# An encoder kernel at 272 tokens: the layer norm between two layers done in place on fp32 sums, its evacuations given priority, weights split in pairs

## The chip, the core and the metric

One Trainium2 chip, one of its cores. TensorE (PE) multiplies, VectorE (DVE), ScalarE (ACT) and GpSimd (POOL) work on tiles of 128 partitions, and DMA queues bring the weights. The metric is the device time of one execution in microseconds (us).

## The reference

Four layers of a post-norm encoder, on 256 tokens and 16 meta tokens, width 2048. The mixers are neighbourhood attention (A), differential attention (B), sliding-window attention with grouped keys (C), and A again. Each takes its projections q, k, v, z from one matrix, gates its output by silu(z) and goes through an output matrix. Everything is fp32.

```python
for i in range(DEPTH):
    y = mixer_i(h, w_in)
    out = jnp.einsum('ble,ed->bld', y, w_out[i])
    h = _layer_norm(DEEPNORM_ALPHA * h + out, ln_g[i], ln_b[i])
```

## The kernel before

Everything is held transposed: features on partitions, 272 tokens along the row, 16 tiles of 128 features (k-tiles). A product of fp32 quality is three matmuls (`mm3`, L148 to L150) of values split into a high part (rounded to fp32r) and the rest: hi·hi, lo·hi, hi·lo. Activations are split where they are made. Weights are streamed from HBM and split on the way: `split_to` takes a granule (4 k-tiles by 128 columns), ACT writes wh (L156), DVE writes wl = raw − wh (L157), both 128x512. The splits run up to 8 granules ahead of PE. A granule is 12 matmuls, an output tile of 128 features 48.

An order of granules is written out by `granules`; `run` walks through it and emits the matmuls of one granule at each step, then one step of each side task (attention of a head, evacuations, residual, norm). From this program a scheduler that simulates the engines sets each engine's queue, so a queue's order isn't the order of the code. PSUM has three banks for accumulators (acc, taken in turn), two for scores and column sums (sc), two for transposes (tr), one for attention outputs (o).

At the end of a layer, `on_out` (L706) adds the residual to an output tile (`residual`: L693 on POOL adds the two halves of h, then ACT scales by alpha). `accum` takes a pivot off, splits d·g into uh and ul (with two more columns that hold the norm's gain and bias, from which the matmul makes two column sums of the weights), and keeps running sums of d and d² on POOL (L753, L754). After the last of the 16 tiles `norm_stats` makes the column sums on PE, then negmu (L776), variance, Ln and Exp on ACT, and one Newton step on DVE, whose last instruction is L784 (rstd).

So that PE needn't wait for that, the first seven input tiles of the next layer (DEFERRED) are multiplied with the un-normalised uh, ul. `rows` corrects them at their evacuation: a copy of the two extra columns (gb, two buffers, L308), an STT on DVE that reads the accumulator and adds negmu times the first (L310), and a multiplication by rstd on POOL (L314). ACT and DVE then write the two halves (for q and k: L322, L332), from which the scores are made. All other input tiles need the normalised h: `normalise` forms it for each k-tile by adding uh and ul on POOL (L797), an STT on DVE (L798), a multiplication by rstd on POOL (L799), and a split on ACT and DVE (L802, L803). `exact` is the mark that the first normalised granule has been reached. At the very end `norm_last` normalises the output with L820 and later lines and stores it.

(An STT is a scalar_tensor_tensor, one DVE instruction with two tensors and a scalar.)

## Time and profile before

| | us |
|---|---|
| median of 3 runs (lowest to highest) | 2007.85 (2006.71 to 2008.03) |
| the profiled execution | 2007.29 |
| its span | 2005.5 |
| PE busy | 1957.6 (98%) |
| DVE busy | 1456.4 (73%) |
| ACT busy | 1105.0 (55%) |
| POOL busy | 677.1 (34%) |

The chain of work that ended last is PE for 93% and DVE for 5%. The mean granted clock of PE is 0.991 of full. Busy times are of the profiled execution; what lies around its span is 1.8 us.

### The profile page before, as it was taken

The page shows a single profiled execution, that of the slowest core. Times are in us where ns is not written, and L with a number is a line of the kernel's source. Part 1 is how long each engine was busy: PE and PEld are TensorE (multiplying, and loading weights), DVE is VectorE, ACT ScalarE, POOL GpSimd, SP SyncE. Part 2 cuts the span into 40 slices and gives each one's busy share as a digit, 9 for nine tenths or more (in the row PEclk, how much of TensorE's full clock was granted, in tenths as well). Part 3 has the DMA queues.
Part 4 walks back from the last instruction along what each step waited for, and adds up shares of the span by engine and source line. Part 5 has one row for each costly group of instructions (what it writes and reads, how often), then busy time and mean ns, then how long its engine had stood idle before and what let it go on. Part 6 is the DMA issues. An engine that isn't in the chain of part 4 may idle for free.

```text
span 2005.5 us, 40741 instructions
## 1 busy us (share of the span) xinstructions
PE 1957.6 (98%) x15794; PEld 1948.7 (97%) x15794; DVE 1456.4 (73%) x2617; ACT 1105.0 (55%) x2396; POOL 677.1 (34%) x947
## 2 busy tenths in 40 slices
PE   9999999999989999999999899999998999999995
PEld 9999999999989999999999899999998999999995
DVE  7666666667998777777779977766898666666665
ACT  6555555555656555555555655655555555555553
POOL 2110011118683122212396832324965111111084
PEclk9999999999999999999999999999999999999998
DMA  8444454444534444444445344444444444445442
GB/s 277 172 155 176 155 176 155 173 148 160 199 121 154 149 167 148 167 155 160 154 151 188 109 163 150 148 151 172 149 172 155 171 167 170 171 176 175 159 165 78
DMA packets 52466, 324.00 MB, mean 162 GB/s; under 512 B 5904, under 2 KB 12064, under 8 KB 14768
## 3 DMA queue, kind: packets, MB, share of 16 engines
q1 hardware_dynamic: 51984, 320.76, 44.8%
q8 instruction: 124, 2.03, 0.4%
q14 instruction: 70, 0.57, 0.1%
q0 software_dynamic: 288, 0.63, 0.1%
HBM read 319.27 MB, written 2.10 MB: 160 GB/s over the span
## 4 chain that ended last, share of the span: by engine, by line
PE 93%; DVE 5%; issue 1%; POOL 1%; DMA 0%; ACT 0%; SPq 0%; DVEq 0%; POOLq 0%
PE acc L148 28%; PE acc L150 28%; PE acc L149 28%; DVE wl L157 1%; PE sc L150 1%; PE sc L148 1%; PE sc L149 1%; PE o L150 1%; PE o L149 1%; DVE ht L798 1%; PE o L148 1%; PE tr L464 1%; PE tr L472 1%; DVE yl L803 0%; DVE yl L822 0%
## 5 line engine op out<-in xcount | busy, mean ns | idle before, releaser
L157 DVE TENSOR_TENSOR wl<-raw,wh 128x512 fp32r<-128x512 f32 x1184 | 904.2, 770 | 435.8 <-ACT wh L156 424.0
L156 ACT CAST wh<-raw 128x512 fp32r<-128x512 f32 x1184 | 721.8, 618 | 609.8 <-PE acc L149 584.6
L148 PE MATMUL acc<-yh,wh 128*128 128x272 f32 (+2 forms) x2448 | 702.1, 287 | 0.0
L149 PE MATMUL acc<-yl,wh 128*128 128x272 f32 (+2 forms) x2448 | 701.8, 287 | 0.0
L150 PE MATMUL acc<-yh,wl 128*128 128x272 f32 (+2 forms) x2448 | 700.7, 286 | 0.0
L148 PE MATMUL acc<-hh,wh 128*128 128x272 f32 (+3 forms) x2288 | 664.8, 291 | 5.4 <-ACT wh L156 5.3
L150 PE MATMUL acc<-hh,wl 128*128 128x272 f32 (+3 forms) x2288 | 663.7, 290 | 0.2 <-DVE wl L157 0.2
L149 PE MATMUL acc<-hl,wh 128*128 128x272 f32 (+3 forms) x2288 | 662.5, 290 | 1.0 <-DVE hl L157 1.0
L148 PEld LDWEIGHTS acc<-yh,wh 128*128 128x128 f32 x2448 | 461.0, 188 | 0.3
L149 PEld LDWEIGHTS acc<-yl,wh 128*128 128x128 f32 x2448 | 460.9, 188 | 0.1
L150 PEld LDWEIGHTS acc<-yh,wl 128*128 128x128 f32 x2448 | 460.7, 188 | 0.0
L148 PEld LDWEIGHTS acc<-hh,wh 128*128 128x128 f32 x2288 | 434.7, 190 | 6.1 <-ACT wh L156 5.8
L149 PEld LDWEIGHTS acc<-hl,wh 128*128 128x128 f32 x2288 | 433.8, 190 | 1.3 <-DVE hl L157 1.3
L150 PEld LDWEIGHTS acc<-hh,wl 128*128 128x128 f32 x2288 | 434.1, 190 | 0.5 <-DVE wl L157 0.4
L346 DVE RECIPROCAL ez<-ez 128x272 f32<-128x272 f32 (+1 forms) x64 | 116.7, 1824 | 24.4 <-POOL ez L344 24.4
L347 POOL TENSOR_TENSOR gate<-gate,ez 128x272 f32<-128x272 f32 (+1 forms) x64 | 66.0, 1031 | 109.8 <-DVE ez L346 107.8
L407 POOL MEMSET vs<- 128x16 f32 x32 | 3.6, 113 | 236.5 <-PE tr L472 215.1
L344 POOL TENSOR_SCALAR ez<-ez 128x272 f32<-128x272 f32 (+1 forms) x64 | 27.3, 427 | 162.0 <-ACT ez L343 161.8
L419 POOL MEMSET s<- 128x16 f32 x32 | 3.6, 114 | 191.8 <-PE tr L469 163.2
L754 POOL TENSOR_TENSOR os<-os,sq 128x272 f32<-128x272 f32 (+1 forms) x59 | 62.9, 1066 | 0.0
L799 POOL TENSOR_TENSOR ht<-ht,rstd 128x272 f32<-128x272 f32 x48 | 50.9, 1073 | 26.2 <-DVE rstd L784 15.6
L753 POOL TENSOR_TENSOR os<-os,r 128x272 f32<-128x272 f32 x45 | 47.7, 1060 | 20.0 <-DVE r L706 20.0
(278 smaller groups left out, 2095.8 us busy)
## 6 DMA issues: line engine op xcount, KB each, us to landing
raw<-in_wts SPq DMA_DIRECT2D x293, 1024.0 KB, 4.8
bias<-in_bias_a SPq DMA_DIRECT2D x32, 184.0 KB, 2.3
raw<-in_wts SPq DMA_DIRECT2D x12, 256.0 KB, 5.4
yh<-in_xT SPq DMA_DIRECT2D x16, 136.0 KB, 4.9
out_h<-raw SPq DMA_DIRECT2D x8, 256.0 KB, 2.1
dist<-in_dist_b POOLq DMA_DIRECT2D x1, 272.0 KB, 6.9
dist<-in_dist_c POOLq DMA_DIRECT2D x1, 272.0 KB, 4.8
lnp<-in_lnp POOLq DMA_DIRECT2D x1, 64.0 KB, 4.2
```

The source lines that it names most:

```text
L148: mm(out, lhsT=lh, rhs=rh, start=start, stop=False)
L149: mm(out, lhsT=lh, rhs=rl, start=False, stop=False)
L150: mm(out, lhsT=ll, rhs=rh, start=False, stop=stop)
L156: nc.scalar.copy(out=hi, in_=src)
L157: nc.vector.tensor_sub(out=lo, in0=src, in1=hi.bitcast(F32))
L344: nc.gpsimd.tensor_scalar(out=view(ez), in0=view(ez), scalar1=1.0, scalar2=1.0, op0=ALU.mult, op1=ALU.add)
L346: nc.vector.reciprocal(view(ez), view(ez))
L347: nc.gpsimd.tensor_tensor(out=view(zc), in0=view(zc), in1=view(ez), op=ALU.mult)
L464: nc.tensor.transpose(tr[:96, at[c]:at[c] + 128], s[:, c // 2, c % 2 * 96:c % 2 * 96 + 96], ident)
L753: nc.gpsimd.tensor_tensor(out=view(self.s1), in0=view(self.s1), in1=d, op=ALU.add)
L754: nc.gpsimd.tensor_tensor(out=view(self.s2), in0=view(self.s2), in1=sq, op=ALU.add)
L799: nc.gpsimd.tensor_tensor(out=t, in0=t, in1=whole(rstd), op=ALU.mult)
```

## The change

- The sums d of a layer stay in fp32 in 16 tiles of their own, one per k-tile, and are normalised in place: POOL adds negmu (L829, 16 a layer, in place of the 32 of L797 and L799), DVE multiplies by gain and rstd (L831, held behind Newton's last step), and the split follows as before (L835 on DVE).
- The residual is made in place from the same tiles by one STT on DVE (L719) or one ACT instruction (L721); POOL's addition of the halves is gone. `on_out` also adds alpha times the norm's bias (L733 is that addition).
- The two column sums are split together and have priority in the scheduler, and so have the statistics and `rows`. The running sums of the last tile are on DVE (L780, L781). The square of the mean is read from PSUM. The STT of `rows` (now L332) is held behind Newton's last step.
- Attention of deferred tiles waits for the mark `exact`.
- From the fourth weight chunk on, splits are of two granules (128x1024, now L166 and L167) into five buffers of that size in place of nine.
- hi and lo of an activation are in one tile, so one copy writes the extra columns of both. Tile order of layer C, numbers of buffers, and the queue of six small loads (POOL's before, ACT's now) change too.

```diff
-SETS = (("hh", "hl"), ("yh", "yl"))
-BUFS = {"raw": 3, "wh": LOOKAHEAD + 1, "wl": LOOKAHEAD + 1, "qh": 2, "ql": 2, "kh": 2, "kl": 2,
...
+BUFS = {"raw": 3, "wh": LOOKAHEAD // PAIR + 1, "wl": LOOKAHEAD // PAIR + 1, "qh": 2, "ql": 2, "kh": 2, "kl": 2,
         "vs": 2, "ez": 1, "gate": 3, "bias": 2, "s": 3, "nm": 4, "sm": 4, "nm2": 4, "sm2": 4,
-        "ph": 1, "pl": 1, "pm": 1, "vm": 2, "ht": 5, "r": 4, "gb": 2, "vh": 2, "vl": 2,
+        "ph": 1, "pl": 1, "pm": 1, "vm": 2, "ht": 3, "gb": 2, "vh": 2, "vl": 2,
...
-            t += [(("k", g), 16 + g), (("v", g), 20 + g)]
...
+            if g == 0:
+                order = [("k", 0), ("v", 0), ("k", 1), ("v", 1)] + order
+            elif g < 3:
+                order[4:4] = [("k", g + 1), ("v", g + 1)]
+            t += [((n, i), {"q": 0, "k": 16, "v": 20, "z": 24}[n] + i) for n, i in order]
...
+    def undeferred(self, key):
+
+        if key in self.deferred:
+            yield from self.need("exact", 0)
...
-            src = self.raw[i // CHUNK][:, i % CHUNK]
-            wh = self.st([128, GRAN, 128], F32R, "wh")
-            wl = self.st([128, GRAN, 128], F32R, "wl")
-            self.hilo(src, wh, wl)
-            self.split.append((wh, wl))
-            if i % CHUNK == 0:
+            g = i % CHUNK
+            wh = self.st([128, PAIR, GRAN, 128], F32R, "wh")
+            wl = self.st([128, PAIR, GRAN, 128], F32R, "wl")
+
+            step = 1 if i < 3 * CHUNK else PAIR
+            for a in range(0, PAIR, step):
+                self.hilo(self.raw[i // CHUNK][:, g + a:g + a + step], wh[:, a:a + step], wl[:, a:a + step])
+            self.split += [(wh[:, a], wl[:, a]) for a in range(PAIR)]
...
-        nc.gpsimd.dma_start(out=self.lnp, in_=lnp)
+        nc.scalar.dma_start(out=self.lnp, in_=lnp)
+        nc.gpsimd.tensor_scalar_mul(self.lnb, self.lnp[:, :, :, 1], ALPHA)
...
-        nc.vector.tensor_copy(out=gb, in_=wide(acc)[:, NTOK:])
         t = self.tok(F32, "ht")
-        nc.vector.scalar_tensor_tensor(out=view(t), in0=view(negmu), scalar=gb[:, 0:1], in1=view(acc),
-                                       op0=ALU.mult, op1=ALU.add)
-        if scale:
-            nc.gpsimd.tensor_scalar_mul(gb[:, 1:2], gb[:, 1:2], scale)
-        nc.gpsimd.tensor_tensor(out=view(t), in0=view(t), in1=view(rstd_q if scale else rstd), op=ALU.mult)
+        with self.tc.high_priority():
+            nc.vector.tensor_copy(out=gb, in_=wide(acc)[:, NTOK:])
+            with self.tc.issue_after(self.newton.ins):
+                nc.vector.scalar_tensor_tensor(out=view(t), in0=view(negmu), scalar=gb[:, 0:1], in1=view(acc),
+                                               op0=ALU.mult, op1=ALU.add)
+            if scale:
+                nc.gpsimd.tensor_scalar_mul(gb[:, 1:2], gb[:, 1:2], scale)
+            nc.gpsimd.tensor_tensor(out=view(t), in0=view(t), in1=view(rstd_q if scale else rstd), op=ALU.mult)
...
     def residual(self, l, m, view):
 
         nc = self.nc
-        t = self.tok(F32, "ht")
-        self.hres[m], self.pre[m] = t, False
-        h = view(t)
-        nc.gpsimd.tensor_tensor(out=h, in0=view(self.uh[m]).bitcast(F32), in1=view(self.ul[m]).bitcast(F32), op=ALU.add)
-        yield
-        nc.scalar.activation(h, h, AF.Copy, scale=ALPHA)
-        yield
-        if ("piv", l) in self.ready:
-            nc.gpsimd.tensor_tensor(out=h, in0=h, in1=view(self.piv), op=ALU.subtract)
-            self.pre[m] = True
+        h = view(self.d[m])
+        self.pre[m] = ("piv", l) in self.ready
+        if self.pre[m]:
+            nc.vector.scalar_tensor_tensor(out=h, in0=h, scalar=ALPHA, in1=view(self.piv), op0=ALU.mult, op1=ALU.subtract)
+        else:
+            nc.scalar.activation(h, h, AF.Copy, scale=ALPHA)
+        return
+        yield
...
-        self.d[m] = self.tok(F32, f"{SETS[l % 2][1]}{m}" if last else "r")
         r = view(self.d[m])
-        nc.vector.tensor_add(r, view(self.hres[m]), view(acc))
+        if l:
+            nc.vector.scalar_tensor_tensor(out=r, in0=view(acc), scalar=self.lnb[:, l - 1, m:m + 1], in1=r,
+                                           op0=ALU.add, op1=ALU.add)
+        else:
+            nc.vector.tensor_add(r, r, view(acc))
...
-            uh, ul = (self.tok(F32R, f"{n}{m}") for n in SETS[l % 2])
+            uh, ul, gb = self.pair(l % 2, m)
...
-            for u, c in ((uh, self.lnh), (ul, self.lnl)):
-                nc.gpsimd.tensor_copy(out=wide(u)[:, NTOK:], in_=c[:, l, m].bitcast(F32))
+            nc.gpsimd.tensor_copy(out=gb, in_=self.lnhl[:, l, m].bitcast(F32))
...
-            nc.gpsimd.tensor_tensor(out=view(self.s1), in0=view(self.s1), in1=d, op=ALU.add)
-            nc.gpsimd.tensor_tensor(out=view(self.s2), in0=view(self.s2), in1=sq, op=ALU.add)
+            eng = nc.gpsimd if m < KT - 1 else nc.vector
+            eng.tensor_tensor(out=view(self.s1), in0=view(self.s1), in1=d, op=ALU.add)
+            eng.tensor_tensor(out=view(self.s2), in0=view(self.s2), in1=sq, op=ALU.add)
...
-            p1 = yield from self.column_sums(self.s1, view)
-            p2 = yield from self.column_sums(self.s2, view)
-        yield
+            p1, p2 = self.ptok("sc"), self.ptok("sc")
+            with self.tc.high_priority():
+                for p, s, tags in ((p1, s1, ("sumh", "suml")), (p2, s2, ("rsx", "rsy"))):
+                    h, lo = (view(self.tok(F32R, n)) for n in tags)
+                    self.hilo(s, h, lo)
+                    nc.tensor.matmul(view(p), lhsT=self.ones_r, rhs=h, start=True, stop=False)
+                    nc.tensor.matmul(view(p), lhsT=self.ones_r, rhs=lo, start=False, stop=True)
...
+        with self.tc.high_priority():
+            nc.scalar.activation(t, view(p1), AF.Square, scale=1.0 / D)
+            nc.vector.tensor_scalar_mul(negmu, view(p1), -1.0 / D)
...
-            t = whole(self.tok(F32, "ht"))
-            nc.gpsimd.tensor_tensor(out=t, in0=whole(self.uh[k]).bitcast(F32), in1=whole(self.ul[k]).bitcast(F32), op=ALU.add)
-            nc.vector.scalar_tensor_tensor(out=t, in0=whole(negmu), scalar=g, in1=t, op0=ALU.mult, op1=ALU.add)
-            nc.gpsimd.tensor_tensor(out=t, in0=t, in1=whole(rstd), op=ALU.mult)
-            yield
-            self.nh[k], self.nl[k] = (self.tok(F32R, f"{n}{k}") for n in SETS[l % 2])
+            t = whole(self.d[k])
+            nc.gpsimd.tensor_tensor(out=t, in0=t, in1=whole(negmu), op=ALU.add)
+            with self.tc.issue_after(self.newton.ins):
+                nc.vector.scalar_tensor_tensor(out=t, in0=t, scalar=g, in1=whole(rstd), op0=ALU.mult, op1=ALU.mult)
+            yield
+            self.nh[k], self.nl[k], _ = self.pair(l % 2, k)
```

DVE, first seam (the handover from layer A to layer B): the evacuation of the third deferred tile. Before, where acc_7398 is the third tile's accumulator:

```order
L308 COPY gb_7512<-acc_7398 128x2
L332 SCALAR_TENSOR_TENSOR kl_7420<-ht_7391,gb_7389,kh_7419 128x272
L798 SCALAR_TENSOR_TENSOR ht_7445<-negmu_7261,lnp_233,ht_7445 128x272
L157 TENSOR_TENSOR wl_7608<-raw_7307,wh_7607 128x512
L803 SCALAR_TENSOR_TENSOR yl_1410_7412<-ht_7381,lnp_233,yh_1409_7411 128x272
L798 SCALAR_TENSOR_TENSOR ht_7469<-negmu_7261,lnp_233,ht_7469 128x272
L157 TENSOR_TENSOR wl_7637<-raw_7307,wh_7636 128x512
L310 SCALAR_TENSOR_TENSOR ht_7514<-negmu_7261,gb_7512,acc_7398 128x272
L803 SCALAR_TENSOR_TENSOR yl_1418_7442<-ht_7415,lnp_233,yh_1417_7441 128x272
```

It stood behind nine steps of normalisation. Of the change, where acc_6619 is the third tile's (and acc_6708 the fourth's):

```order
L835 SCALAR_TENSOR_TENSOR y_1008_6765<-d_16_86,lnp_209,y_1008_6765 128x272
L167 TENSOR_TENSOR wl_6847<-raw_6645,wh_6846 128x1024
L835 SCALAR_TENSOR_TENSOR y_1011_6786<-d_17_87,lnp_209,y_1011_6786 128x272
L330 COPY gb_6702<-acc_6619 128x2
L167 TENSOR_TENSOR wl_6883<-raw_6734,wh_6882 128x1024
L835 SCALAR_TENSOR_TENSOR y_1015_6809<-d_18_88,lnp_209,y_1015_6809 128x272
L330 COPY gb_6791<-acc_6708 128x2
L537 ISA s_7012,nm_7013<-sc_7017,bias_6587 128x272
L537 ISA nm_7013 128x1
L537 ISA s_7012,nm_7013<-sc_7046,bias_6587 128x272
L537 ISA nm_7013 128x1
L332 SCALAR_TENSOR_TENSOR ht_6703<-negmu_6446,gb_6702,acc_6619 128x272
```

The last L835 of the sixteen, two weight splits and the softmax rows (L537) stand ahead of it now; its column copy (L330) is eight rows ahead of it.

PE, same seam: where a deferred tile takes a bank late. Before, where acc_7759 is the sixth tile and acc_7866 the seventh, in the bank that the fourth (acc_7522) had:

```order
L148 MATMUL acc_7759<-hh_1352_7169,wh_7636 128x274
L149 MATMUL acc_7759<-hl_1353_7170,wh_7636 128x274
L150 MATMUL acc_7759<-hh_1352_7169,wl_7637 128x274
L148 MATMUL acc_7866<-hh_1180_6235,wh_7665 128x274
L149 MATMUL acc_7866<-hl_1181_6236,wh_7665 128x274
L150 MATMUL acc_7866<-hh_1180_6235,wl_7666 128x274
```

Of the change, where acc_6796 is the fifth tile, sc are the scores of the first head, and acc_6867 is the sixth tile, in the bank that acc_6619 had:

```order
L159 MATMUL acc_6796<-h_947_6411,wh_6681 128x274
L160 MATMUL acc_6796<-h_947_6411,wl_6682 128x274
L158 MATMUL sc_7017<-kh_6637,qh_6610 128x272
L158 MATMUL sc_7046<-kh_6637,qh_6610 128x272
L159 MATMUL sc_7017<-kl_6638,qh_6610 128x272
L160 MATMUL sc_7017<-kh_6637,ql_6611 128x272
L159 MATMUL sc_7046<-kl_6638,qh_6610 128x272
L160 MATMUL sc_7046<-kh_6637,ql_6611 128x272
L158 MATMUL sc_7066<-kh_6637,qh_6610 16x272
L159 MATMUL sc_7066<-kl_6638,qh_6610 16x272
L160 MATMUL sc_7066<-kh_6637,ql_6611 16x272
L158 MATMUL acc_6867<-h_852_5629,wh_6730 128x274
```

The nine score matmuls of the first head stand in one row between the fifth and the sixth tile; before, the scores of this seam stood in pieces within the fourth, the fifth and the seventh tile.

POOL, same seam: the row behind the running sums of the last tiles. Before, with L799 (rstd) first, L797 (adding the halves) and L314 (evacuation) between:

```order
L754 TENSOR_TENSOR os_6021<-os_6021,sq_7175 128x272
L313 TENSOR_SCALAR gb_7353<-gb_7353 128x1
L799 TENSOR_TENSOR ht_7275<-ht_7275,rstd_7262 128x272
L799 TENSOR_TENSOR ht_7299<-ht_7299,rstd_7262 128x272
L799 TENSOR_TENSOR ht_7325<-ht_7325,rstd_7262 128x272
L799 TENSOR_TENSOR ht_7349<-ht_7349,rstd_7262 128x272
L314 TENSOR_TENSOR ht_7355<-ht_7355,rstdq_7263 128x272
L797 TENSOR_TENSOR ht_7381<-hh_1199_6330,hl_1200_6331 128x272
L797 TENSOR_TENSOR ht_7415<-hh_1203_6344,hl_1204_6345 128x272
L314 TENSOR_TENSOR ht_7391<-ht_7391,rstd_7262 128x272
L797 TENSOR_TENSOR ht_7445<-hh_1218_6427,hl_1219_6428 128x272
```

Of the change, the last of sixteen L829 (they begin right behind the running sums), then the evacuations:

```order
L829 TENSOR_TENSOR d_15_85<-d_15_85,negmu_6446 128x272
L829 TENSOR_TENSOR d_16_86<-d_16_86,negmu_6446 128x272
L829 TENSOR_TENSOR d_17_87<-d_17_87,negmu_6446 128x272
L829 TENSOR_TENSOR d_18_88<-d_18_88,negmu_6446 128x272
L335 TENSOR_SCALAR gb_6581<-gb_6581 128x1
L336 TENSOR_TENSOR ht_6582<-ht_6582,rstdq_6448 128x272
L336 TENSOR_TENSOR ht_6615<-ht_6615,rstd_6447 128x272
L335 TENSOR_SCALAR gb_6702<-gb_6702 128x1
L336 TENSOR_TENSOR ht_6703<-ht_6703,rstdq_6448 128x272
```

The multiplications for the first deferred tiles (L336) stood among those of the normalisation and stand behind all sixteen additions now.

## Rows read from the trace of the kernel before

**Rows 1.** Windows, all engines: window, length, busy us (instructions) of each engine, clock.

```profile
core 0: us, PE busy (x) PEld busy (x) DVE busy (x) ACT busy (x) POOL busy (x), PEclk, DMA share, GB/s
...
480.00:560.00 80.00, 79.97 (x641) 79.68 (x639) 70.52 (x99) 47.06 (x98) 63.48 (x72) 1.00 0.49 177
560.00:620.00 60.00, 51.25 (x383) 50.23 (x384) 56.78 (x102) 34.33 (x80) 39.53 (x43) 0.94 0.37 125
...
1095.00:1150.00 55.00, 47.51 (x355) 44.85 (x354) 54.78 (x105) 31.38 (x77) 48.68 (x59) 0.97 0.31 116
...
1490.00:1540.00 50.00, 42.70 (x316) 41.32 (x315) 48.37 (x82) 27.22 (x63) 37.74 (x41) 0.93 0.35 125
1540.00:1900.00 360.00, 360.00 (x3002) 360.00 (x3001) 228.42 (x409) 189.62 (x393) 36.99 (x66) 1.00 0.49 172
```

**Rows 2.** Timeline of PE, first seam: start, us, operation, [idle before it <-releaser].

```profile
533.87 0.29 PE L148 MATMUL acc<-hh,wh 128*128 128x274 f32 x1
...
561.60 0.39 PE L149 MATMUL sc<-kl,qh 128*128 128x272 f32 x1 [1.63 <-DVE kl L332]
...
580.42 0.57 PE L148 MATMUL acc<-hh,wh 128*128 128x274 f32 x1 [4.33 <-ACT wh L156]
...
581.24 0.43 PE L148 MATMUL acc<-hh,wh 128*128 128x274 f32 x1
581.47 0.43 PE L149 MATMUL acc<-hl,wh 128*128 128x274 f32 x1
...
589.77 0.28 PE L148 MATMUL acc<-yh,wh 128*128 128x272 f32 x1
```

**Rows 3.** Timeline of DVE, first seam, behind Newton's step.

```profile
559.37 1.26 DVE L157 TENSOR_TENSOR wl<-raw,wh 128x512 fp32r<-128x512 f32 x1
...
561.47 0.49 DVE L798 SCALAR_TENSOR_TENSOR ht<-negmu,lnp,ht 128x272 f32<-128x272 f32 x1
...
564.41 0.68 DVE L157 TENSOR_TENSOR wl<-raw,wh 128x512 fp32r<-128x512 f32 x1
...
573.30 1.01 DVE L798 SCALAR_TENSOR_TENSOR ht<-negmu,lnp,ht 128x272 f32<-128x272 f32 x1
...
579.79 0.49 DVE L310 SCALAR_TENSOR_TENSOR ht<-negmu,gb,acc 128x272 f32<-128x272 f32 x1
```

**Rows 4.** Groups by line, DVE, 540 to 610: shapes xcount | busy us, mean ns | idle before.

```profile
L157 DVE TENSOR_TENSOR wl<-raw,wh 128x512 fp32r<-128x512 f32 x35 | 31.5, 906 | 0.5 <-ACT wh L156 0.5
L803 DVE SCALAR_TENSOR_TENSOR yl<-ht,lnp,yh 128x272 fp32r<-128x272 f32 x16 | 11.9, 753 | 0.0
```

**Rows 5.** Groups by line, POOL, 540 to 610.

```profile
L799 POOL TENSOR_TENSOR ht<-ht,rstd 128x272 f32<-128x272 f32 x16 | 17.5, 1105 | 7.1 <-DVE ht L798 4.0 <-DVE rstd L784 2.7 <-DVE sm L517 0.4
L797 POOL TENSOR_TENSOR ht<-hh,hl 128x272 f32<-128x272 f32 x12 | 13.2, 1108 | 1.4 <-DVE yl L803 1.0 <-DVE sm L518 0.4
```

**Rows 6.** Timeline of DVE, first seam, the statistics.

```profile
536.16 0.42 DVE L706 TENSOR_TENSOR r<-ht,acc 128x272 f32<-128x272 f32 x1
...
539.23 0.43 DVE L157 TENSOR_TENSOR suml<-os,sumh 128x272 fp32r<-128x272 f32 x1
...
541.14 0.43 DVE L776 TENSOR_SCALAR negmu<-sc 128x272 f32<-128x272 f32 x1
...
548.05 0.43 DVE L784 SCALAR_TENSOR_TENSOR rstd<-rst,rstd 128x272 f32<-128x272 f32 x1
```

**Rows 7.** Windows, two short stretches of the first seam.

```profile
533.87:552.79 18.92, 18.92 (x150) 18.86 (x149) 18.35 (x32) 11.80 (x25) 7.70 (x10) 1.00 0.55 203
580.00:590.00 10.00, 9.58 (x56) 9.61 (x57) 10.00 (x17) 4.29 (x9) 7.55 (x7) 0.71 0.35 127
```

**Rows 8.** Timeline of ACT, the start.

```profile
5.17 0.62 ACT L156 CAST wh<-raw 128x512 fp32r<-128x512 f32 x1 [1.88 <-DMA raw<-in_wts]
```

**Rows 9.** DMA issues, the start: queue, count, KB, median us to landing.

```profile
lnp<-in_lnp POOLq DMA_DIRECT2D x1, 64.0 KB, 4.2
```

**Rows 10.** Timeline of ACT, the end.

```profile
1984.75 0.42 ACT L777 ACTIVATE rst<-negmu 128x256 f32<-128x256 f32 x1 [0.75 <-DVE negmu L776]
```

More of the change, by code (lines that the diff above doesn't have):

```diff
@@ L68, in in_tiles @@
             h = 4 * g
-            t += [(("k", g), 16 + g), (("v", g), 20 + g)]
             order = [("q", h), ("q", h + 1), ("z", h), ("q", h + 2), ("z", h + 1),
                      ("q", h + 3), ("z", h + 2), ("z", h + 3)]
-            t += [((n, i), i if n == "q" else 24 + i) for n, i in order]
+            if g == 0:
[3 more added lines that the diff above has]
+            t += [((n, i), {"q": 0, "k": 16, "v": 20, "z": 24}[n] + i) for n, i in order]
     return t
@@ L141, in tok, with pair @@
         return self.st([128, 2, 144], dt, tag)
+    def pair(self, s, k):
+        t = self.st([128, 2, 2, 144], F32R, f"{SETS[s]}{k}")
+        return t[:, 0], t[:, 1], t.rearrange("p s a b -> p s (a b)")[:, :, NTOK:NTOK + 2]
     def ptok(self, tag):
@@ L240, in setup @@
             nc.tensor.matmul(warm[:, :128], lhsT=self.ones, rhs=self.ones, start=True, stop=True)
-        self.uh, self.ul, self.d, self.hres, self.pre = ([None] * KT for _ in range(5))
-        x = [self.tok(F32, f"yh{k}") for k in range(KT)]
+        self.uh, self.ul, self.d, self.pre = ([None] * KT for _ in range(4))
+        x = self.d = [self.tok(F32, f"d{k}") for k in range(KT)]
         for kc in range(KT // GRAN):
@@ L352, in finish @@
         nc = self.nc
-        yh, yl = (self.tok(F32R, f"{n}{k}") for n in SETS[1 - self.layer % 2])
+        yh, yl, _ = self.pair(1 - self.layer % 2, k)
         nc.scalar.copy(out=view(yh), in_=view(y))
@@ L421, in attn_a @@
             s2 = self.meta_tile()
+        yield from self.undeferred(("q", h))
         qh, ql = yield from self.need(("q", h), 2)
@@ L497, in attn_b @@
         for j in range(2):
+            yield from self.undeferred(("q", 2 * h + j))
             qh, ql = yield from self.need(("q", 2 * h + j), 2)
@@ L606, in vt_c @@
         nc = self.nc
+        yield from self.undeferred(("v", g))
         vs = yield from self.need(("v", g), 2)
@@ L628, in attn_c @@
         nm2, sm2 = self.st([META, 1], F32, "nm2"), self.st([META, 1], F32, "sm2")
+        yield from self.undeferred(("q", h))
         qh, ql = yield from self.need(("q", h), 2)
@@ L845, in run @@
                 self.dist = self.st([128, 2, NTOK], F32, "dist")
-                nc.gpsimd.dma_start(out=self.dist, in_=self.dist_in[kind])
+                nc.scalar.dma_start(out=self.dist, in_=self.dist_in[kind])
             gridded = last and kind == "A"
```

39 lines of the change are left out of this document (21 added, 18 removed).

## Prediction

> **What bounds the kernel now.** I read the busy time of each engine by stage first [rows 1]. In the long stretches TensorE (PE) is busy throughout, 360.00 us of 360 in the last, so nothing there can be won by a faster split or a shorter VectorE (DVE) queue. It has holes in three places, each where one layer's last output tile hands over to the next layer: 60 − 51.25 = 8.75 us, 55 − 47.51 = 7.49 us and 50 − 42.70 = 7.30 us, together 23.5 us. I call these the seams. There DVE is busy for 56.78 of 60, 54.78 of 55 and 48.37 of 50 us: everybody waits for it. The granted clocks are 0.94, 0.97 and 0.93; with levels at 2.4 and 1.2 GHz that is 60 × 0.06 × 2 + 55 × 0.03 × 2 + 50 × 0.07 × 2 = 17.5 us at 1.2 GHz.
>
> Then the queue of PE in the first seam [rows 2]. The last output tile ends at 533.87, which I call T0. Seven deferred tiles follow, and the first normalised tile starts at 589.77, T0 + 55.9. In between PE waits, among others, 1.63 us for kl and 4.33 us at 580.42. The profile puts the latter down to a weight split on ScalarE (ACT). I read it otherwise: there are three acc banks, the seventh deferred tile takes the bank of the fourth, and DVE evacuates that one (L310) at 579.79 [rows 3], 0.6 us before PE goes on. So it is a bank that DVE came to late. After it PE runs at 0.23 us a matmul (581.24 to 581.47) instead of 0.13, the 1.2 GHz level.
>
> Why is DVE late? The same instruction has two durations there [rows 3]: a normalisation step of 128x272 takes 0.49 or 1.01 us, a weight split of 128x512 0.68 or 1.26 us. The long form comes where GpSimd (POOL) runs a tensor_tensor from SBUF beside it; an evacuation from PSUM keeps its 0.49. The means over 540 to 610 are 753 and 906 ns [rows 4]; by them 32 × 0.26 (L798 and L803 alike) + 35 × 0.23 = 16 us of DVE time are contention, over about 40 POOL operations, 28 of them in two groups [rows 5]: 0.4 us for each on average, 0.52 for one that meets a step fully.
>
> **The change, part by part.** *POOL's work.* In each seam 32 tensor_tensors of the normalisation become 16, and the residual adds (L693) go. The 16 are not spread: POOL's new order has them in one row directly behind negmu, which is there at T0 + 7.3 now (541.14, [rows 6]) and will be at about T0 + 7. At 1.1 us each [rows 5] they end at about T0 + 25. The multiplications for the first two deferred tiles stand behind all sixteen, so the first q and k are complete at T0 + 26 to 27.
>
> *The statistics.* Newton's last step ends at 548.48 now, T0 + 14.6, and the last on_out of a layer starts at T0 + 2.3 [rows 6]. After the change 17 DVE rows lead from that one to Newton's step, 8.8 us by the durations below; that gives T0 + 11.1, and with two steps on ACT and a weight split ahead of one of them I take T0 + 13.2 (12.3 to 13.9). The gain is 1.4 us.
>
> *The splits by pairs.* The trace has no 128x1024 split. A plain tensor_tensor takes 0.43 us with 272 elements [rows 6] and 0.68 with 512 [rows 3], so 512 more add 0.53 to a spacing of 0.61 (0.68 less the overlap with the next): I take 1.16 us alone, near this end, against 1.22 for two single ones; the bounds are 1.14 and 1.22 alone, 1.7 and 2.36 beside POOL (one addition of 0.52 to 0.58, or two). Outside the seams a full PE covers it; inside, seven pairs gain at most 7 × 0.08 = 0.6 us. ACT's half is covered: 34.33 of 60 us busy [rows 1].
>
> *The deferred tiles.* This part decides. DVE's new order puts the evacuations of the first two deferred tiles directly behind Newton's step, but that of the third behind all sixteen L831, all sixteen L835 and two softmax rows: its copy of two columns needs a free gb buffer, and the two are held until ql is written. PE's new order has the sixth deferred tile in the third one's bank, so PE can't begin the sixth before that evacuation. From Newton's step to its end DVE has, in the first seam: 7 pairs × 1.16 = 8.1, 32 normalisation steps × 0.41 (0.49 less the overlap) = 13.1, two ql/kl steps 0.8, three evacuations 1.2, the rest 1.0; in sum 24.2 us without contention (23.0 and 24.0 in the other seams). POOL has 11.8 us of its adds left when Newton ends, some 10, and two multiplications: 12 × 0.48, between average and full meeting, = 5.8 us. The evacuation ends at T0 + 13.2 + 24.2 + 5.8 = T0 + 43.2. PE would get there after 253 matmuls of 0.1278 (18.92 us for 148; two of the 150 in that row had begun before, [rows 7]), at T0 + 32.3. A wait for kl ahead of the scores, whose step is late in the same queue, takes part of the difference; it doesn't add. So PE loses 10.9 us here, 9.7 and 10.7 in the other two: 31.3. Behind it all normalised tiles are ready, and attention of the deferred tiles comes later, so I find no second stall.
>
> *What that replaces.* Idle 23.5 us; each wait costs 0.16 us more than its bracket, since the matmul ahead lasts 0.29 at a spacing of 0.13, and I count nineteen waits in the three seams ([rows 2] show two), 3.0 us; the 17.5 us at 1.2 GHz lose 1 − 0.128/0.23 = 0.44 of themselves, 7.7 us. In sum 34.2 us. Of the clock to come: around the wait of 4.33 us, 5.8 us of one window were at 1.2 GHz (0.71 over 10 us, [rows 7]); in the whole second seam, with shorter waits, 3.3 us. That is 1.5 to 3.0 us lost a seam; I take 2.2, 6.6 in all. New sum 31.3 + 6.6 = 37.9, so +3.7.
>
> *On the port.* The rows say that a POOL operation of 1.1 us costs a DVE step 0.52, half of itself. The Trainium skill ("SBUF — State Buffer", section "Who interferes with whom") has a harder rule: the ports that DVE shares with GpSimd are an exclusive lock. By it a DVE step would wait for the whole operation; rows 3 show half of that.
>
> *Head.* The small loads go from POOL's queue to ACT's. ACT now waits for lnp ahead of its first weight cast, PE for lam ahead of its first matmul. That cast starts at 5.17 now [rows 8]; lnp lands 4.2 us after its issue [rows 9]. Issued at about 2 us and landing in 2 to 4.2, it puts the cast at 5.2 to 6.8 with ACT's own work: 0 to +1.6. POOL's adds that ran beside DVE there go: −1. I take +0.5 (−1 to +2). *Tail.* The Square reads PSUM and no longer waits for negmu (0.42 us on ACT behind it, [rows 10]); the three L820 ahead of L782 stay in the new order. −0.4.
>
> *Moved or free.* L719 and L730 on DVE in place of adds on POOL and DVE: DVE is busy for 70.52 of 80 us in an output stage, PE for 79.97 [rows 1], and the splits run up to 8 granules ahead, 96 matmuls or 12 us. The largest burst in the new order, behind the pivot, is 14 operations or 7 us: covered. Without the cover it would cost those 7 us a layer at most.
>
> Sum: 2007.3 (this profiled run's own time, 0.6 us under the median of 2007.85) + 3.7 + 0.5 − 0.4 = 2011.1.
>
> **The rivals.** *The bank is free early (faster).* If the adds run at 0.97 and mostly before Newton's step, or meet PSUM reads only, contention halves or goes: the evacuation ends at T0 + 40.3 or 37.4, PE loses 8.0 or 5.1 us, the clock 1.5. Three seams, the second 1.2 and the third 0.2 shorter: 3 × 9.5 − 1.4 = 27.1, a gain of 7, 2000; or 3 × 6.6 − 1.4 = 18.4, a gain of 16, 1991.5. For it: half of POOL's seam work is gone, and DVE's uncontended work leaves only 5 us of wait. Against: the adds stand in one row when nine L831 stand in one row too.
>
> *Two waits with two slow stretches (slower).* The wait for kl and that for the bank are nine matmuls apart, so PE stands still nearly throughout. If Newton ends at T0 + 13.9, pairs beside POOL take 2.3 us, and the clock stays low for 6.8 us, the evacuation ends at T0 + 45.5 and a seam costs 13.2 + 3.0: 48.6 − 1.4 = 47.2, +13, 2020. It decides from T0 + 44 on. For it: 4.33 us of waiting already brought a long slow stretch. Against: POOL is through at T0 + 25.
>
> *The lock holds for whole operations (slower).* Then a POOL operation costs 1.1 us: 12 × 1.1 instead of 5.8, +7.4 a seam, +22, 2033. No 128x272 step took over 1.01 us [rows 3], against it. It is what the Trainium skill's rule ("SBUF — State Buffer") would give.
>
> *The change doesn't do what it says.* The priority doesn't reach the third tile's evacuation: DVE's order shows that, so it is part of the forecast.
>
> **How the numbers follow.** Forecast case (2004 to 2016) 0.52, bank early 0.27, two slow stretches 0.18, the lock 0.03. A measurement of this kernel can tell about 0.2%, 4 us, from no change: 2003.8 to 2011.9 is "same". Faster 0.27; of the forecast case 0.32 lies under 2011.9: same 0.32; slower 0.20 + 0.21 = 0.41. The predicted time is the forecast's sum, rounded to 2011.0. The range from 1996 to 2021 leaves out a third of the early case, the upper end of the slow one and the lock, under 0.2.
>
> **What would show it.** In the trace after: Newton's step at T0 + 13; POOL's sixteen adds in a row to T0 + 25; holes of PE of 9 to 11 us ahead of the sixth deferred tile, with the scores between them, ended by the third tile's evacuation; none at the seventh; a stretch at 1.2 GHz behind. The prediction is wrong if the holes are under 7 us (contention over-estimated), if DVE's steps beside POOL are not near 0.93 apart, or if PE stops in the output stages or for over 2 us more at the start.

## The result, and the profile after

The changed kernel takes 2022.98 us (median of 4 runs, 2022.68 to 2025.39), the kernel before 2007.94 beside it: a ratio of 1.0079, 95% interval 1.0061 to 1.0096. It is 15 us slower. The forecast was 2011.0, slower by 3, with a range that ended at 2021.

The first page of the profile after, its span and busy times:

```profile
span 2021.0 us, 38521 instructions
PE 1959.6 (97%) x15794; PEld 1953.1 (97%) x15794; DVE 1355.7 (67%) x2077; ACT 990.8 (49%) x1774; POOL 518.5 (26%) x735
```

DVE, ACT and POOL have 101, 114 and 159 us less to do than before, and yet the kernel is slower. The windows of the three seams after, in the columns of [rows 1] (window, length, busy us and instructions of PE, PEld, DVE, ACT, POOL, then the granted clock):

```profile
560.00:600.00 40.00, 28.43 (x203) 27.33 (x202) 33.63 (x63) 22.28 (x42) 10.19 (x13) 0.83 0.37 132
...
1105.00:1140.00 35.00, 22.68 (x167) 22.29 (x166) 28.63 (x52) 18.56 (x34) 9.05 (x13) 0.80 0.36 126
...
1500.00:1540.00 40.00, 27.38 (x201) 26.90 (x200) 33.84 (x65) 20.93 (x42) 8.19 (x12) 0.83 0.40 141
```

PE is idle for 11.6, 12.3 and 12.6 us there, 36.5 in all against 23.5 before. What it waits for, over the whole kernel (us in total, times, longest):

```profile
PE acc L158 <- DVE ht L332: 16.2, 2, 10.9
PE sc L159 <- DVE kl L354: 14.2, 2, 7.3
PE sc L158 <- DVE nm L537: 4.7, 1, 4.7
```

The many small waits of before have become six, two a seam, and all but one of the six are in this list (the sixth is 1.44 us for v_mid). In the first seam, where T0 is now 536.96, the timeline of PE shows the scores wait for kl and then, for their third part, for a softmax row that stands directly ahead of the third tile's evacuation; [rows 2] had 4.33 us at the seventh tile there:

```profile
536.96 0.29 PE L158 MATMUL acc<-h,wh 128*128 128x274 f32 x1
...
575.31 0.60 PE L159 MATMUL sc<-kl,qh 128*128 128x272 f32 x1 [6.88 <-DVE kl L354]
...
581.27 0.41 PE L158 MATMUL sc<-kh,qh 128*16 128x272 f32 x1 [4.69 <-DVE nm L537]
```

And DVE's and POOL's timelines of the same seam (the rows that answer to [rows 3, 5, 6]): Newton's last step, eight L831 in a row, the end of that queue with kl, and the third tile's evacuation, the first of the two L332 at 581.50; and POOL's sixteen additions in one row.

```profile
551.26 0.90 DVE L816 SCALAR_TENSOR_TENSOR rstd<-rst,rstd 128x272 f32<-128x272 f32 x1
...
555.47 7.03 DVE L831 SCALAR_TENSOR_TENSOR d<-d,lnp,rstd 128x272 f32<-128x272 f32 x8
...
574.77 0.48 DVE L354 SCALAR_TENSOR_TENSOR kl<-ht,gb,kh 128x272 fp32r<-128x272 f32 x1
...
581.50 0.89 DVE L332 SCALAR_TENSOR_TENSOR ht<-negmu,gb,acc 128x272 f32<-128x272 f32 x2
```

```profile
546.04 15.74 POOL L829 TENSOR_TENSOR d<-d,negmu 128x272 f32<-128x272 f32 x16 [11.90 <-DVE negmu L809]
```

So the hole is where the forecast had it, and by the mechanism it named. It isn't the whole loss. In the long stretches PE is busy throughout in both kernels, and yet not equally fast. A window in the output stage of the first layer, full in both, of before and then of after:

```profile
460.00:520.00 60.00, 60.00 (x488) 60.00 (x487) 46.51 (x61) 35.54 (x74) 54.13 (x68) 1.00 0.44 162
```

```profile
460.00:520.00 60.00, 60.00 (x476) 60.00 (x476) 50.10 (x56) 30.38 (x47) 30.50 (x29) 1.00 0.48 170
```

Both have 60.00 of 60 us at a clock of 1.00, but 488 matmuls in the one and 476 in the other: 123 ns a matmul against 126. "Busy" doesn't say how fast; the count beside it does. In the last layer, from 1600 to 1900, it is 2503 before and 2478 after:

```profile
1600.00:1900.00 300.00, 300.00 (x2503) 300.00 (x2502) 189.85 (x337) 158.40 (x330) 31.01 (x55) 1.00 0.49 171
```

```profile
1600.00:1900.00 300.00, 300.00 (x2478) 300.00 (x2478) 169.29 (x243) 136.12 (x230) 34.14 (x54) 1.00 0.47 169
```

### The profile page after: what moved, and what is told of

The parts are those of the page before. It is cut to its first block, busy times and chain, and to the rows that moved or that the text cites. A ratio compares the mean times of both kernels' runs of the same rounds, so it can differ in the third digit from the quotient of the medians.

```text
span 2021.0 us, 38521 instructions
## 1 busy us (share of the span) xinstructions
PE 1959.6 (97%) x15794; PEld 1953.1 (97%) x15794; DVE 1355.7 (67%) x2077; ACT 990.8 (49%) x1774; POOL 518.5 (26%) x735
## 4 chain that ended last, share of the span: by engine, by line
PE 92%; DVE 4%; DMA 1%; ACT 1%; issue 1%; POOL 0%; SPq 0%; DVEq 0%
PE acc L158 28%; PE acc L160 28%; PE acc L159 28%; DVE wl L167 1%; DVE d L831 1%; DMA raw<-in_wts 1%; PE sc L160 1%; PE sc L159 1%; PE sc L158 1%; PE o L159 1%; PE o L160 1%; PE o L158 1%; PE tr L487 1%; PE tr L495 1%; ACT wh L166 0%
## 5 line engine op out<-in xcount | busy, mean ns | idle before, releaser
L167 DVE TENSOR_TENSOR wl<-raw,wh 128x1024 fp32r<-128x1024 f32 (+1 forms) x598 | 752.6, 1259 | 466.7 <-ACT wh L166 463.4
L166 ACT CAST wh<-raw 128x1024 fp32r<-128x1024 f32 (+1 forms) x598 | 619.5, 1038 | 543.6 <-PE acc L159 492.3
L158 PE MATMUL acc<-y,wh 128*128 128x272 f32 (+2 forms) x2448 | 708.4, 289 | 10.9 <-DVE ht L332 10.9
L159 PE MATMUL acc<-y,wh 128*128 128x272 f32 (+2 forms) x2448 | 703.8, 288 | 0.0
L160 PE MATMUL acc<-y,wl 128*128 128x272 f32 (+2 forms) x2448 | 701.8, 287 | 0.0
L158 PE MATMUL acc<-h,wh 128*128 128x272 f32 (+3 forms) x2288 | 660.6, 289 | 7.2 <-DVE ht L332 5.3
L159 PE MATMUL acc<-h,wh 128*128 128x272 f32 (+3 forms) x2288 | 661.3, 289 | 0.1
L160 PE MATMUL acc<-h,wl 128*128 128x272 f32 (+3 forms) x2288 | 660.8, 289 | 0.2 <-DVE wl L167 0.2
L158 PEld LDWEIGHTS acc<-y,wh 128*128 128x128 f32 x2448 | 461.9, 189 | 11.2 <-issue 11.0
L160 PEld LDWEIGHTS acc<-y,wl 128*128 128x128 f32 x2448 | 462.0, 189 | 0.2
L159 PEld LDWEIGHTS acc<-y,wh 128*128 128x128 f32 x2448 | 461.9, 189 | 0.1
L158 PEld LDWEIGHTS acc<-h,wh 128*128 128x128 f32 x2288 | 432.4, 189 | 8.7 <-issue 6.0
L159 PEld LDWEIGHTS acc<-h,wh 128*128 128x128 f32 x2288 | 432.9, 189 | 0.6 <-DVE h L167 0.3
L160 PEld LDWEIGHTS acc<-h,wl 128*128 128x128 f32 x2288 | 432.8, 189 | 0.4 <-DVE wl L167 0.4
L780 POOL TENSOR_TENSOR os<-os,d 128x272 f32<-128x272 f32 (+1 forms) x56 | 64.5, 1151 | 94.2 <-DVE d L730 59.3
L467 ACT ACTIVATE s<-s,nm 128x192 f32<-128x192 f32 x64 | 28.6, 446 | 76.1 <-DVE nm L459 76.1
L781 POOL TENSOR_TENSOR os<-os,sq 128x272 f32<-128x272 f32 (+1 forms) x56 | 62.3, 1112 | 7.0 <-ACT sq L775 6.7
```

Source lines behind the costliest of these rows:

```text
L158: mm(out, lhsT=lh, rhs=rh, start=start, stop=False)
L159: mm(out, lhsT=lh, rhs=rl, start=False, stop=False)
L160: mm(out, lhsT=ll, rhs=rh, start=False, stop=stop)
L166: nc.scalar.copy(out=hi, in_=src)
L167: nc.vector.tensor_sub(out=lo, in0=src, in1=hi.bitcast(F32))
L467: nc.scalar.activation(p[t], p[t], AF.Exp, bias=nm[:, t:t + 1], scale=-1.0, accum_out=sm[:, t:t + 1])
```

## The experiments

Two theories were on trial for the two losses. For the holes: the third deferred tile's evacuation stands behind nearly all of the normalisation. For the slower matmuls: the addresses of the activations in SBUF. The change put the two halves of a k-tile into one tile of 2304 bytes a partition, 18 times 128. The traces hold no addresses; where a tile lies follows from sizes and the order of allocation in the code. By that every hi of y now lies at an even and every lo at an odd multiple of 128 bytes (of h the other way round). Before, single tiles of 9 times 128 bytes lay such that in y successive operands alternated: hi even, lo odd, hi even, then in the next k-tile hi odd, lo even, hi odd.

**One more gb buffer.**

```diff
-        ... "ht": 3, "gb": 2, ...
+        ... "ht": 3, "gb": 3, ...
```

> The changed kernel with three gb buffers in place of two, nothing else. Theory (the third deferred tile's evacuation stands behind nearly all of the normalisation because its column copy has no buffer): the copy gets its buffer, DVE's order has this evacuation about 7 us of work earlier in each seam, and the holes of PE (12.8, 12.9, 13.6 us) shrink by 4 to 7 us each; about 2005 us (2000 to 2010). Rival (the holes belong to DVE's whole queue: what comes early for one wait is late for the next): the seventh tile or the scores wait instead, under 2 us a seam are won, 2018 to 2023.

2007.97 us (2006.87 to 2009.78): 15.0 us less than the changed kernel, ratio to before 1.0001 (0.9992 to 1.0010). The waits of PE in it:

```profile
PE acc L158 <- DVE ht L332: 20.2, 3, 7.1
```

One wait a seam is left, of about 6.7 us, where there were two of 12 together; the scores don't wait any more, because the scheduler let the sixth tile go ahead of most of them. This is the theory. The clock recovers too: the stretch at 1.2 GHz is 6.8 us in each seam instead of 13.7. The seam is not empty, because the evacuation is only 6 to 7 us of work further ahead: in the first seam it ends 22.8 us after Newton's step, in the changed kernel 29.8.

**No additions on POOL** (the additions of negmu in the normalisation are left out).

```diff
-            nc.gpsimd.tensor_tensor(out=t, in0=t, in1=whole(negmu), op=ALU.add)
```

> The changed kernel without L829, POOL's sixteen additions of negmu in each seam (this part of the computation is left out). Theory (POOL's additions cost DVE about 0.5 us for each operation that meets one): DVE's steps in the seams keep 0.41 us of spacing throughout, Newton's step ends 1 to 1.5 us earlier and the third evacuation 6 to 8 us earlier; with the hole ending that much earlier three seams give back 18 to 24 us: 1999 to 2005. Rival (the contention is small beside DVE's own queue): 2 us a seam, 2017.

1990.96 us (1990.55 to 1991.82), 32 us less, more than either theory gave. The groups by line of DVE in the first seam, with the additions (the changed kernel) and without:

```profile
L831 DVE SCALAR_TENSOR_TENSOR d<-d,lnp,rstd 128x272 f32<-128x272 f32 x16 | 11.9, 782 | 0.0
L835 DVE SCALAR_TENSOR_TENSOR y<-d,lnp,y 128x272 fp32r<-128x272 f32 x16 | 7.4, 488 | 0.0
```

```profile
L830 DVE SCALAR_TENSOR_TENSOR d<-d,lnp,rstd 128x272 f32<-128x272 f32 x16 | 7.4, 519 | 0.0
L834 DVE SCALAR_TENSOR_TENSOR y<-d,lnp,y 128x272 fp32r<-128x272 f32 x16 | 7.0, 487 | 0.0
```

The mean of an L831 falls from 782 to 519 ns; L835, which runs when POOL is through, doesn't change. Newton's last three steps, 0.93, 0.90 and 0.90 us beside the additions, take 0.43 to 0.44; the last of them without:

```profile
549.86 0.44 DVE L816 SCALAR_TENSOR_TENSOR rstd<-rst,rstd 128x272 f32<-128x272 f32 x1
```

The price of contention is as forecast, about half of a POOL operation; that it also lies on the statistics was not in the forecast. The rest of the 32 us isn't contention alone: without the additions the scheduler made another order, with the third evacuation 3 to 7 us of work further ahead (two to five weight splits fewer stand before it). So this run gives the price of an operation but not, by its time, what the additions cost.

**Halves exchanged in odd k-tiles.** The operands of successive matmuls then alternate between even and odd multiples of 128 bytes everywhere. The orders of PE and POOL are the same but for names; DVE and ACT each have one instruction more in the head, since the gain and bias columns are split in two calls.

```diff
-        return t[:, 0], t[:, 1], t.rearrange(...)[:, :, NTOK:NTOK + 2]
+        return t[:, k % 2], t[:, 1 - k % 2], t.rearrange(...)[:, :, NTOK:NTOK + 2]
...
-        self.hilo(self.lnp, self.lnhl[:, :, :, 0], self.lnhl[:, :, :, 1])
+        for a in range(2):
+            self.hilo(self.lnp[:, :, a::2], self.lnhl[:, :, a::2, a], self.lnhl[:, :, a::2, 1 - a])
```

> The changed kernel with high and low half of the 16 odd k-tiles exchanged inside their tiles, so that the operands of successive matmuls alternate between addresses that are even and odd in units of 128 bytes, as they did in the kernel before in its output stages. Nothing else moves. Theory (the spacing of matmuls outside the seams depends on where the moving operands lie: 126.5 ns in the output stage of the first layer after the change, 123.4 before): spacing there falls to about 123.5 ns, and the time by 5 to 10 us, to 2013 to 2018. Rival (spacing depends on something else, as the weights' layout): no change within 1 us.

2011.21 us (2010.07 to 2012.39), 11.8 us less; a little more than the theory's upper end. The same window as above:

```profile
460.00:520.00 60.00, 60.00 (x489) 60.00 (x488) 52.17 (x57) 31.62 (x49) 32.58 (x31) 1.00 0.50 177
```

489 matmuls, one more than before the change. The seams are as they were: PE's six waits there are 36.6 us, against 36.5.

**Small loads on POOL's queue again** (lnp, lam, gcol, sink and the two dist; dma_start of nc.gpsimd in place of nc.scalar).

> The changed kernel with the six small loads on POOL's queue again, as before. Theory (on ACT's queue they are in the way of the first weights and of ACT's first casts; the head is 1.6 us longer): 1.5 us less, 2021.5. Rival (the head's loss is due to the residual scaling on ACT): no change at the head.

2022.52 us (2021.49 to 2022.81), 0.5 less, which these runs can't tell from nothing, nor from the theory's 1.5. The head itself decides. The 192nd matmul on an accumulator, before, in the changed kernel and in this one:

```profile
34.22 0.29 PE L150 MATMUL acc<-hh,wl 128*128 128x272 f32 x1
```

```profile
35.84 0.29 PE L160 MATMUL acc<-h,wl 128*128 128x272 f32 x1
```

```profile
33.95 0.29 PE L160 MATMUL acc<-h,wl 128*128 128x272 f32 x1
```

It starts 1.9 us earlier than in the changed kernel and 0.3 earlier than before; in the other nine traces with the loads on ACT's queue it starts between 35.28 and 37.32. So the head's loss belongs to the queue, and the rival (no change at the head) falls. The time doesn't follow because 1.4 us of the gain are lost again in the first seam and the second layer; on what is open.

**The kernel before with other addresses.** If the addresses are the cause, they must do the same to a kernel that has neither joint tiles nor pairs. First the alternation where it lacked it (hh and hl), then the changed kernel's pattern where it had the better one (yh and yl). In both no instruction of any engine moves.

```diff
-                self.uh[k], self.ul[k] = self.tok(F32R, f"hh{k}"), self.tok(F32R, f"hl{k}")
+                self.uh[k], self.ul[k] = (self.tok(F32R, f"{n}{k}") for n in (SETS[0] if k % 2 else SETS[0][::-1]))
+                if k % 2 == 0:
+                    self.uh[k], self.ul[k] = self.ul[k], self.uh[k]
```

> The kernel before with the tiles hh and hl of the even k-tiles allocated in the other order, so that the moving operands alternate between even and odd multiples of 128 bytes in layers A and C as they do in its other stages; no instruction moves. Theory (addresses of the moving operands set the spacing): the spacing in the first layer falls by about 1 ns a matmul as it did in the changed kernel with the exchange (122.06 to 120.87 on average), 3 to 6 us less in all: 2002 to 2005. Rival (what the exchange gave belongs to the joint tiles of the changed kernel): no change, 2007.9 within 1.

2004.83 us (2003.19 to 2005.80), ratio 0.9985 (0.9976 to 0.9994): 2.8 us faster than before, at the weak end of what was expected. One row of it speaks against the theory as it stands. In the output stage of the first layer PE reads y, whose addresses this edit leaves alone, and there it holds 482 matmuls where the kernel before had 488:

```profile
460.00:520.00 60.00, 60.00 (x482) 60.00 (x481) 47.59 (x62) 34.54 (x72) 53.87 (x63) 1.00 0.43 159
```

```diff
-        x = [self.tok(F32, f"yh{k}") for k in range(KT)]
+        x = []
+        for k in range(KT):
+            self.tok(F32, f"yl{k}")
+            x.append(self.tok(F32, f"yh{k}"))
```

> The kernel before with yl allocated ahead of yh, k-tile by k-tile, so that every yh lies at an even and every yl at an odd multiple of 128 bytes, as the joint tiles y of the changed kernel do; no instruction of any engine moves. Theory (those addresses cost the changed kernel its slower spacing): the output stages of the first and third layer go from 123.4 and 124.8 ns to 126.5, the last layer gets 1 to 2 ns slower at 256 columns; 3 to 8 us more, 2011 to 2016. Rival (addresses don't matter, the joint tile does): 2007.6 within 1.

2014.56 us (2013.72 to 2015.88), ratio 1.0038 (1.0024 to 1.0052): 7.2 us slower than before by a change of addresses alone. Its windows, the output stage of the first layer and the last layer:

```profile
460.00:520.00 60.00, 60.00 (x476) 60.00 (x475) 46.45 (x61) 35.69 (x74) 53.73 (x67) 1.00 0.44 157
```

```profile
1600.00:1900.00 300.00, 300.00 (x2482) 300.00 (x2481) 187.24 (x338) 157.28 (x326) 28.80 (x53) 1.00 0.49 171
```

476 and 2482: the counts of the changed kernel (476 and 2478), in the kernel before. So joint tiles aren't needed for them, against the rival. But the expectation had the output stage of the third layer slower as well, from 124.8 to 126.5 ns, and it is not. PE reads the same y tiles there, and each has a single buffer and so stays in its place. From 1400 to 1460 in the kernel before, in this one, in the changed kernel and in the one with exchanged halves:

```profile
1400.00:1460.00 60.00, 60.00 (x482) 60.00 (x481) 49.32 (x64) 35.40 (x75) 55.73 (x64) 1.00 0.45 162
```

```profile
1400.00:1460.00 60.00, 60.00 (x485) 60.00 (x484) 48.18 (x63) 35.53 (x75) 54.82 (x65) 1.00 0.47 166
```

```profile
1400.00:1460.00 60.00, 60.00 (x476) 60.00 (x475) 51.60 (x56) 30.38 (x48) 32.15 (x30) 1.00 0.48 171
```

```profile
1400.00:1460.00 60.00, 60.00 (x489) 60.00 (x488) 53.94 (x57) 31.96 (x50) 33.84 (x31) 1.00 0.52 177
```

The two kernels with joint tiles hold 476 and 489 in both layers. The two with single tiles hold 488 and 476 in the first, but 482 and 485 here. So it is shown that a change of addresses alone changes the spacing and costs 7.2 us. That the parity of 128 bytes is what counts is not shown: it fits the joint tiles and the first layer, and fails here and in the row of 482 above.

**Evacuations ahead of the normalisation.** Here the order is forced instead of left to a buffer: `rows` keeps its STTs in a list, and `normalise` holds L831 from k = 6 on and L835 from the start behind the third of them, L835 from k = 7 on behind the fourth. With the exchange of halves, and seven gb buffers.

```diff
+            n = (k >= 6)
+            while n and len(self.evac) < 3:
+                yield
-            with self.tc.issue_after(self.newton.ins):
+            with self.tc.issue_after(self.evac[2].ins if n else self.newton.ins):
                 nc.vector.scalar_tensor_tensor(out=t, in0=t, scalar=g, in1=whole(rstd), op0=ALU.mult, op1=ALU.mult)
...
+            n = (k >= 0) + (k >= 7)
+            while n and len(self.evac) < n + 2:
+                yield
+            with self.tc.issue_after(self.evac[n + 1].ins if n else self.newton.ins):
                 nc.vector.scalar_tensor_tensor(out=whole(self.nl[k]), in0=t, scalar=b, ...)
```

> The changed kernel with the exchange of halves, seven gb buffers, and the normalisation of later k-tiles held behind the evacuations of the third (L831 from k = 6 on, L835) and the fourth deferred tile (L835 from k = 7 on). Theory (the holes are evacuations that stand behind normalisation in DVE's queue, and DVE has the time for both): the hole ahead of the sixth tile goes, 0 to 4 us a seam remain ahead of the seventh or of the normalised tiles, of 13; 2011.2 less 27 to 36: 1975 to 1985. Rival (DVE is simply full in a seam, the wait moves to the normalised tiles): 8 us or more a seam remain, 1996 or more.

1980.96 us (1980.25 to 1981.33), ratio to before 0.9868 (0.9854 to 0.9881): 42 us less than the changed kernel, 27 less than the one before, in the middle of what the theory gave. Its first seam and its longest waits:

```profile
555.00:600.00 45.00, 41.83 (x328) 40.69 (x327) 44.09 (x80) 28.83 (x56) 20.28 (x19) 1.00 0.44 164
```

```profile
PE acc L160 <- DVE wl L167: 5.5, 6, 1.7
PE acc L158 <- ACT wh L166: 1.9, 3, 0.8
PE acc L158 <- DVE ht L333: 1.6, 2, 0.8
```

PE idles 3 us instead of 12, the clock stays at 1.00, and the work that ran in the hole was there all along: DVE is busy for 44.09 of 45 us here. The same parts of the change that made it slower in the order it came in make it the fastest kernel of this study in another order, with the halves exchanged. What each of the three edits gives of it this run doesn't say.

**Attention of deferred tiles not held back** (`undeferred` returns at once).

> The changed kernel with attention of the deferred tiles let loose again (no waiting for the mark exact). Theory (the holes are made by the third evacuation; attention has no part in it, and fills them with a few matmuls at most): within 3 us of the changed kernel, 2020 to 2026. Rival (holding attention back took work out of the holes that could have filled them): 5 us or more faster.

2023.02 us (2021.88 to 2023.64), the changed kernel's time. Holding attention back neither costs nor gains anything as long as the holes are there.

**Single splits** (PAIR = 1).

> The changed kernel with splits of one granule (128x512) again. Theory (pairs save DVE under 1 us a seam and nothing elsewhere): within 3 us, 2020 to 2027. Rival (pairs hold up what stands behind them, in the statistics above all, where DVE waits for ACT's pair): Newton's step comes 1 us earlier and the time falls by 3 us or more.

2020.89 us (2020.00 to 2021.70), 2.1 us less: by the time the theory's case; but the mechanism is the rival's, and larger than it said. Newton's last step ends at 549.81 in this kernel, whose last output tile ends at 537.72: T0 + 12.1 against T0 + 15.2 with pairs. In the other two seams it comes 1.6 us earlier. The time doesn't follow, because most of what Newton's step gains is lost again ahead of the third evacuation: in the first seam 32.0 us lie between the two instead of 29.8, with 15 single splits in place of 7 pairs, and the evacuation ends at T0 + 44.0 instead of T0 + 45.0.

```profile
548.91 0.90 DVE L816 SCALAR_TENSOR_TENSOR rstd<-rst,rstd 128x272 f32<-128x272 f32 x1
```

**On top of the evacuations first.** Two runs: one with the additions of negmu on DVE (nc.vector in place of nc.gpsimd in L829), one with single splits.

> The kernel with the evacuations first, with L829 (adding negmu) on DVE in place of POOL. Theory (a POOL addition costs DVE 0.5 us, a DVE addition 0.41, and Newton's step loses its three contended steps): Newton's step 1 us earlier, L831 at 0.41 apart, and 0 to 2 us less a seam: 1975 to 1981. Rival (the additions mostly met nothing, so DVE gets 16 x 0.41 us more work a seam): 3 us or more slower, 1984 or more.

1983.98 us (1982.59 to 1986.72), 3 us more, at the rival's lower bound; but the order brings the time here, so the run doesn't decide on the price. DVE's new order puts the sixteen additions ahead of Newton's steps, so that these come later instead of earlier, and PE waits for them in each seam (9.3 us in three waits):

```profile
540.72 5.71 DVE L830 TENSOR_TENSOR d<-d,negmu 128x272 f32<-128x272 f32 x16
...
552.51 0.43 DVE L817 SCALAR_TENSOR_TENSOR rstd<-rst,rstd 128x272 f32<-128x272 f32 x1
```

> The kernel with the evacuations first, with splits of one granule (128x512). Theory (single splits get Newton's step earlier by about 1 us as in the changed kernel, where they gave 2 us, and hold the queue up in smaller pieces): 1977 to 1980. Rival (with the holes gone the statistics no longer set the end, and pairs save DVE time): 1981 to 1985.

1981.75 us (1980.41 to 1982.94), the time with pairs: the rival's lower end. With the holes gone, the size of the splits is worth nothing either way.

**Both simple repairs together**, three gb buffers and the exchange.

> The changed kernel with three gb buffers and the exchange of halves together, no other edit. Theory (two causes that don't touch each other, the evacuation behind the normalisation and the addresses): the gains add, 2023.0 - 15.0 - 11.8 = 1996.2, within 2. Rival (both act on the same waits in part): 2000 or more.

1992.99 us (1991.99 to 1995.12), ratio to before 0.9929 (0.9913 to 0.9946). The gains add, so the two causes are separate ones. It is 3 us less than the sum of 1996.2, beyond the 2 that were expected; but the interval is 6.6 us wide and doesn't tell this from the sum.

## Why the prediction was wrong

**What held.** That PE has holes at these places, and that they end with DVE's evacuation of the third tile: right, shown by the row of L332 (in the first seam the last wait is for the softmax row directly ahead of it) and by one more buffer, which took 15 us away. From Newton's step to that evacuation the forecast had 24.2 + 5.8 = 30.0 us; the trace has 552.1 to 582.0, 29.9, and 28.6 and 29.6 in the other seams (28.8 and 29.8). POOL's sixteen additions in a row to T0 + 25: they end at 561.8, T0 + 24.8. The clock after the holes: 2.2 us a seam were forecast; PE was busy for 5.43, 3.20 and 5.21 us at half clock, which costs 0.44 of each, 6.1 us in all against 6.6 (by the same measure 6.9 before the change). No stall behind: right. The rival of the lock fell, by the 0.90 to 1.0 us that a step beside POOL takes.

**The rival that came nearest.** "Two waits with two slow stretches" gave 2020, and what it names was there in the first seam: two waits, and the third evacuation at T0 + 45.0, beyond its mark of T0 + 44. Its terms were not: it had Newton's step at T0 + 13.9 (measured T0 + 15.2), pairs beside POOL at 2.3 us (1.72 and 1.79), a clock that costs 3.0 us a seam (2.0), and nothing for the long stretches. That its time lies within 3 us of the measured one is luck.

**Step one that failed: Newton's step at T0 + 13.2.** It ends at 552.1, T0 + 15.2, later than before the change (T0 + 14.6), and so in every seam. The forecast took a start at T0 + 2.3, which was a wait of before: on_out now starts at T0 + 0.2, as DVE's timeline shows.

```profile
537.16 0.44 DVE L733 TENSOR_TENSOR d<-d,acc 128x272 f32<-128x272 f32 x1 [0.86 <-PE acc L160]
```

From there 10.9 us were allowed, and it took 15.0. DVE waits 3.8 us of that for weight splits on ACT (its waits from 537 to 552):

```profile
DVE wl L167 <- ACT wh L166: 3.8, 3, 1.6
```

These are the pairs, of which the forecast said that ACT's half is covered by ACT's idle time. It was priced by an average over 60 us ([rows 1]) and not at the place: in a chain of statistics where pairs stand between the steps, the wait for one delays all behind it. ACT did have the time. It stood idle ahead of the first two of the three casts that DVE waited for, the first time by the profile for PE, the second for a reason that the profile doesn't show; the cast just began too late:

```profile
540.09 1.05 ACT L166 CAST wh<-raw 128x1024 fp32r<-128x1024 f32 x1 [0.90 <-PE acc L159]
...
543.30 1.05 ACT L166 CAST wh<-raw 128x1024 fp32r<-128x1024 f32 x1 [1.85 <-issue]
```

Single splits gave 3.1 us of it back (T0 + 12.1) in this seam, 1.6 in the others. Another 1.4 us are Newton's three steps at 0.9 us beside POOL's additions. The forecast counted the additions that are left when Newton's step ends, and forgot those that run beside it. Two us later in each of three seams match, in sum, the 6.2 us by which the idle time, 36.5 us, is over the forecast's 31.3 less 1.0 for the brackets. Seam by seam the match is loose: 1.0, 2.9 and 2.2 us.

**Step two that failed: in the long stretches PE is busy throughout, "so nothing there can be won by a faster split or a shorter VectorE (DVE) queue".** It was taken for "and nothing lost". The term is missing from the sum altogether: the change also moved the operands. How large it is, by two pairs of kernels. With alternating addresses in both: 2011.21 against 2004.83, the change costs 6.4 us. With its own addresses in y in both: 2022.98 against 2014.56, 8.4 us. As it was: 15.0. So 7 to 9 of the 15 us are addresses, and 6 to 8 the seams with whatever else there is, against 3.8 in the forecast's sum.

The traces give a second measure. Both kernels have 15794 matmuls, so one can ask how much later the same-numbered one starts. By that the changed kernel loses 1.8 us up to the 200th, 8.5 us in the three seams (4400 to 5000, 8600 to 9200, 11500 to 12200) and 5.9 us in the stretches between, and gains 0.8 from the 15000th on. The forecast had +0.5, +3.7, nothing and −0.4. The 5.9 are 7.0 lost from the first layer's output stage on, less 1.1 gained before it, which the forecast didn't have either. The holes by idle time (+13.0), fewer waits (six instead of nineteen, −2.0) and the clock (−0.8) would give 10.2 in the seams instead of 8.5; the difference stays open.

**The rest.** The head was +0.5 in the forecast. The 192nd matmul on an accumulator starts 1.6 us later than before, within the forecast's bounds (−1 to +2), and with the small loads on POOL's queue again 0.3 earlier than before: the queue is the reason.

## What to carry to other kernels

Where an engine is full, divide the window by the count of instructions before saying that nothing changes there: a tile made larger or joined with another moves every address behind it, and here that was about half of the loss. Where a program's order is made by a scheduler, a second buffer that is held a little too long can put an instruction at the end of a queue in spite of its priority; read the order of the changed kernel for whom it lets wait, then price the chain by what stands between its steps, not by averages. And look at whether the order, rather than the work, is at fault before undoing a change: in another order and at other addresses the same work took 2% less time than in the order it came in.
